# The first units of a feed-forward: a store behind the fetches, the third block early, a next unit's product moved up

## The chip, the cores and the metric

The kernel runs on one core of a Trainium2 chip. Its time is the device time of one execution in microseconds (us). The engines are TensorE (PE, with its weight loads as PEld), VectorE (DVE), ScalarE (ACT), GpSimd (POOL) and SyncE (SP), whose queue issues all the transfers spoken of here.

## The reference

One layer of a decoder over 2048 prompt tokens and 64 sample tokens, all in float32: an input projection, windowed attention and gated linear attention, an output projection with a residual, and a feed-forward with a squared ReLU. The change lies where the output projection ends and the feed-forward begins:

```
mix = jnp.einsum('bte,ed->btd', jnp.concatenate([attn.astype(x.dtype), gla_out], axis=-1), w_out)
x = x + rms_norm(mix, g_mix_post)
h = rms_norm(x, g_ffn_pre)
u = jax.nn.relu(jnp.einsum('btd,df->btf', h, w_up))
f = jnp.einsum('btf,fd->btd', u * u, w_down)
x = x + rms_norm(f, g_ffn_post)
```

w_up is 1024 x 4096, w_down 4096 x 1024.

## The kernel before

**Products.** A float32 product is made of three matmuls of a shorter type: each operand is split into a high half (a copy on ScalarE) and a low half (a subtraction on VectorE), and high x high, high x low and low x high are added. Both large products of the feed-forward also save one multiplication in eight: operands are cut into 2 x 2 quarters, sums of quarters are formed, and seven products take the place of eight. The seven blocks of activations are H1 to H7. A product with one of them is 12 matmuls of 128x128 on 128x512 (four slices of the inner dimension, three matmuls each).

**Stages.** The prompt is done in two halves of 1024 tokens (`sb` 0 and 1). For each half the up stage (`up`) runs 16 units (`fc` 0 to 15) of 256 columns of w_up; each forms its seven products and two products for the sample tokens, squares the features, and stores them to memory. Then the down stage (`down`) reads features and weight sums back and multiplies them (bank tiles `dn`).

**Rows.** `residual(i, ...)` finishes a block of 128 rows after the output projection: norm, residual, store to `x1_d` (L1423), norm, transposes on TensorE into two banks (`xnT`, L1523), copies out of them on ScalarE into a tile `ht` (L1528), four sums on VectorE (L1535), and a store of the sums to `h_d` (L1537). That store has 3584 pieces of 512 bytes. Row blocks come in the order 0, 4, 1, 5, ..., 10, 14, 11, 15; two of them share one `ht`, and all `ht` share one place, so the copies of block 11 wait until the store of the pair 10 and 14 has landed. Blocks 10, 14, 11 and 15 belong to the second half (`h_d[1]`); the last of them runs inside unit 0 of the first half (`last_rows`), where its transposes use the two banks that block 11's used.

**Unit 0.** H1 and H2 are kept in place. H5, H7 and H6 are fetched from `h_d[0]` as `hraw` (`fetch_h`, L1549) and split (`load_h`); H3 and H4 are fetched late into the place of their own low halves (L1824) and split there (`split_in_place`). The order of unit 0 is written out in `opening`: after each product p of UP_FIRST = (1, 0, 2, 8, 5, 7, 9, 6, 3, 4) stand the steps of that place (0 and 8 are the sample products, 9 their transposes). Later units use UP_ORDER = (1, 5, 7, 0, 6, 8, 3, 2, 9, 4).

**What sets the order.** `te`, `ac` and `dv` are wrappers that keep TensorE, ScalarE and VectorE in the order in which the program is written; their instructions all show as L130. Work on the bare engines (`split_copy`, L218 and L219, and the row blocks before the last) is placed between by the scheduler. The transfers stand on SP's queue, and `tc.issue_after` puts one behind another. Pools of memory are opened and released like a stack, and a tile that lies where an older one lay waits for that one's last reader.

**Names in the profile.** `ua` to `ue` are the banks of products; `s` are the split sums of weight quarters (`13` and `24` in the code), `t` those sums before the split, `w` the split quarters, `raw` the fetched weights, `st` the unit's features, `sam` the sample bank, `both` its copy, `samq` and `samp` the sample features, `rs`, `rt`, `o0s`, `o1s`, `o0t`, `o1t` the down stage's fetched and split operands. `load_up` fetches weights (L1576), `load_down` the second matrix (L1665).

Of the kernel before, what the change touches and what calls it, by code (L numbers as in the profile page):

```python
# [12 lines left out]
F32 = mybir.dt.float32  # L13
# [8 lines left out]
P = 128  # L22
# [31 lines left out]
H_EARLY, H_LATE = (1, 2), (5, 7, 6, 4, 3)  # L54
# [86 lines left out]
def hybrid_step_kernel(ctx: ExitStack, tc: tile.TileContext, I, O):  # L141
# [1266 lines left out]
    def mixed(i, banks, x, x1, junk, ssq, gpost, pool, scalar=nc.scalar, vector=nc.vector):  # L1408
# [14 lines left out]
        nc.sync.dma_start(x1_d[i], x[:n])  # L1423
# [72 lines left out]

    def residual(i, banks, tensor=nc.tensor, scalar=nc.scalar, vector=nc.vector):
# [21 lines left out]
        for h in range(2):  # L1519
# [8 lines left out]
            scalar.activation(ht[:, (6, 2)[h] if second else h], pt, AF.Copy)  # L1528
# [8 lines left out]
        nc.sync.dma_start(h_d[sb][:, kept, :, q], ht[:, kept])  # L1537
# [3 lines left out]
    def fetch_h(sb, p, home="h"):  # L1541
        h_raws[p] = []
        for k in range(0, KT // 2, 2):
# [5 lines left out]
            nc.sync.dma_start(raw, h_d[sb][:, p - 1, k : k + 2])  # L1549
            h_raws[p].append(raw)  # L1550

    def load_h(sb, p, scalar=nc.scalar, vector=nc.vector):
# [40 lines left out]
    for n, i in enumerate(B_ORDER[2:]):  # L1593
# [9 lines left out]
        if n != 1:  # L1603
            run(residual(*early.pop(0)))
# [18 lines left out]
    fetch_h(0, 6, "tmp")  # L1623
# [54 lines left out]

    def up(sb, fc, before, steps=iter(())):
# [5 lines left out]
        X, Z, Y, V = (bank([P, BT], kind, f"u{kind}_{sb}_{fc}") for kind in ("ab"[first], "c", "ba"[first], "de"[fc % 2]))  # L1685
        sam = bank([P, BT], "b", f"sam_{fc}") if sb == 0 else None
        place = []
# [7 lines left out]
        def product(p):  # L1695
            out = {1: X, 2: X, 5: Z, 3: Z, 7: V, 4: V, 6: Y}[p]
            hi, lo = H[p]
            for k in range(KT // 2):
                for u, (a, b) in enumerate(((0, hi), (0, lo), (1, hi))):
                    te.matmul(  # L1700
                        out, weight(sb, fc, p, a, k), b[:, k], start=p in (1, 5, 7, 6) and k + u == 0,
                        stop=k == KT // 2 - 1 and u == 2, skip_group_check=True,
                    )
# [4 lines left out]
        def taken(p):  # L1708
# [38 lines left out]
        for p in UP_FIRST if first else UP_ORDER:  # L1747
            if 0 < p < 8:
# [7 lines left out]
            if first:  # L1756
                opening(p, taken, ahead)
                if p == 3:
                    squared(s(6))
                continue  # L1760
            if p == 1:
                next(before, None)
                if fc or sb:
# [22 lines left out]
        if sb == 0:  # L1786
            sample_features(fc, sam)
# [401 lines left out]
```

## Time and profile before

| | us |
|---|---|
| median of 3 runs | 2207.52 (2206.16 to 2207.61) |
| the profiled execution | 2206.11 |
| its span, first to last instruction | 2204.0 |
| TensorE busy | 2163.2 (98%) |
| VectorE busy | 1531.4 (69%) |
| ScalarE busy | 1219.1 (55%) |

The mean granted clock of TensorE is 0.996 of full speed. A row in order of time gives start, length, engine, line, operation, the tile written and the tile read, shapes, a count where equal rows are merged, and in brackets the idle time before it and what ended that. Matmul rows overlap: a row of twelve is 2.9 us long, and the next begins 2.7 us after it.

### The profile page before, as it was taken

The page shows a single profiled execution, that of the slowest core. Times are in us where ns is not written, and L with a number is a line of the kernel's source. Part 1 is how long each engine was busy: PE and PEld are TensorE (multiplying, and loading weights), DVE is VectorE, ACT ScalarE, POOL GpSimd, SP SyncE. Part 2 cuts the span into 40 slices and gives each one's busy share as a digit, 9 for nine tenths or more (in the row PEclk, how much of TensorE's full clock was granted, in tenths as well). Part 3 has the DMA queues.
Part 4 walks back from the last instruction along what each step waited for, and adds up shares of the span by engine and source line. Part 5 has one row for each costly group of instructions (what it writes and reads, how often), then busy time and mean ns, then how long its engine had stood idle before and what let it go on. Part 6 is the DMA issues. An engine that isn't in the chain of part 4 may idle for free.

```text
span 2204.0 us, 34115 instructions
## 1 busy us (share of the span) xinstructions
PE 2163.2 (98%) x11784; PEld 1864.7 (85%) x11784; DVE 1531.4 (69%) x3101; ACT 1219.1 (55%) x2626; POOL 263.0 (12%) x418
## 2 busy tenths in 40 slices
PE   8999999999999999899999999999999999999998
PEld 7999989999998888688888887887888888888886
DVE  5888868777775665788888655547676666555566
ACT  5889867566664444555555544435444554444444
POOL 2566512121111100000000000000000000000000
PEclk9999999999999999999999999999999999999999
DMA  6344232214336665768777677758554334766685
GB/s 228 131 137 156 96 106 70 68 64 148 136 125 237 223 208 190 239 228 277 260 261 270 232 236 225 240 182 260 180 195 149 138 144 148 238 201 193 194 269 185
DMA packets 240185, 411.53 MB, mean 187 GB/s; under 512 B 25924, under 2 KB 142124, under 8 KB 235900
## 3 DMA queue, kind: packets, MB, share of 16 engines
q1 hardware_dynamic: 240012, 409.35, 55.9%
q8 instruction: 93, 1.52, 0.3%
q14 instruction: 80, 0.66, 0.1%
HBM read 265.82 MB, written 143.99 MB: 186 GB/s over the span
## 4 chain that ended last, share of the span: by engine, by line
PE 85%; DVE 6%; ACT 4%; DMA 2%; issue 1%; POOL 1%; SPq 0%; DVEq 0%; ACTq 0%; POOLq 0%
PE dn L130 26%; PE gproj L130 10%; PE uc L130 7%; PE ua L130 7%; PE out L1318 6%; PE proj L130 5%; PE ue L130 4%; PE ud L130 4%; PE ub L130 4%; PE av L130 1%; PE sam L130 1%; PE dsam L130 1%; PE o L130 1%; PE pT L130 1%; PE sc L130 1%
## 5 line engine op out<-in xcount | busy, mean ns | idle before, releaser
L130 PE MATMUL dn<-o0t,o0s 128*128 128x512 f32 x896 | 349.3, 390 | 2.8 <-DVE f L1891 1.5
L130 PE MATMUL dn<-o1t,o0s 128*128 128x512 f32 x896 | 349.5, 390 | 0.3 <-DVE o1t L219 0.2
L130 PE MATMUL dn<-o0t,o1s 128*128 128x512 f32 x896 | 349.4, 390 | 0.0
L219 DVE TENSOR_TENSOR o1s<-rs,o0s 128x512 fp32r<-128x512 f32 x224 | 154.7, 691 | 227.8 <-ACT o0s L218 223.7
L218 ACT ACTIVATE o0s<-rs 128x512 fp32r<-128x512 f32 x224 | 141.1, 631 | 305.5 <-PE dn L130 282.3
L130 PE MATMUL gproj<-wg,gxh 128*128 128x384 f32 x1024 | 272.5, 342 | 0.3 <-DVE gp_s L213 0.3
L130 ACT ACTIVATE st<-st 128x512 f32<-128x512 f32 x224 | 141.2, 630 | 140.7 <-DVE st L130 136.6
L130 PEld LDWEIGHTS dn<-o0t,o0s 128*128 128x128 f32 x896 | 168.3, 188 | 40.6 <-DVE f L1891 2.4
L130 PEld LDWEIGHTS dn<-o1t,o0s 128*128 128x128 f32 x896 | 168.2, 188 | 37.0 <-DVE o1t L219 1.1
L130 PEld LDWEIGHTS dn<-o0t,o1s 128*128 128x128 f32 x896 | 168.2, 188 | 35.0
L130 PEld LDWEIGHTS gproj<-wg,gxh 128*128 128x128 f32 x1024 | 183.8, 188 | 4.1 <-issue 3.1
L130 PE MATMUL uc<-H,s 128*128 128x512 f32 x768 | 186.8, 391 | 0.4 <-DVE s L130 0.4
L130 PE MATMUL gproj<-wg,gxl 128*128 128x384 f32 x576 | 186.0, 340 | 0.2 <-DVE gp_s L213 0.2
L130 PE MATMUL ua<-H,w 128*128 128x512 f32 x744 | 179.2, 390 | 0.0
L130 PEld LDWEIGHTS uc<-H,s 128*128 128x128 f32 x768 | 142.9, 188 | 31.2 <-DVE s L130 0.8
L130 PEld LDWEIGHTS ua<-H,w 128*128 128x128 f32 x744 | 139.7, 188 | 29.5
L1318 PE MATMUL out<-wo,mt 128*128 128x512 f32 x680 | 158.6, 392 | 0.0
L219 DVE TENSOR_TENSOR o1t<-rt,o0t 128x512 fp32r<-128x512 f32 x224 | 153.5, 685 | 7.0 <-ACT o0t L218 6.9
L208 POOL TENSOR_TENSOR frs<-rs_v,half 128x1 f32<-128x1 f32 (+1 forms) x13 | 10.1, 787 | 1214.4 <-DVE rs_v L206 694.5
L1318 PEld LDWEIGHTS out<-wo,mt 128*128 128x128 f32 x680 | 126.5, 188 | 26.1
L218 ACT ACTIVATE o0t<-rt 128x512 fp32r<-128x512 f32 x224 | 138.3, 618 | 8.9 <-DMA rt<-t_d 7.2
L130 DVE TENSOR_TENSOR st<-st 128x512 f32<-128x512 f32 x160 | 110.6, 692 | 27.0 <-ACT st L130 22.6
(405 smaller groups left out, 4322.3 us busy)
## 6 DMA issues: line engine op xcount, KB each, us to landing
s_d<-st SPq DMA_DIRECT2D x32, 1792.0 KB, 8.7
rs<-s_d SPq DMA_DIRECT2D x224, 256.0 KB, 2.8
raw<-in_w_up SPq DMA_DIRECT2D x64, 512.0 KB, 4.3
rt<-t_d SPq DMA_DIRECT2D x128, 256.0 KB, 4.1
rt<-in_w_down SPq DMA_DIRECT2D x96, 256.0 KB, 3.1
t<-in_w_down SPq DMA_DIRECT2D x64, 256.0 KB, 4.0
t_d<-t SPq DMA_DIRECT2D x32, 512.0 KB, 3.2
hraw<-h_d SPq DMA_DIRECT2D x20, 512.0 KB, 5.1
```

The costliest lines, as they stand in the source:

```text
L130: ins = call(*a, **k)
L208: nc.gpsimd.tensor_tensor(out, v[:n], e, op=ALU.pow)
L218: nc.scalar.activation(hi, src, AF.Copy)
L219: vector.tensor_tensor(lo, src, f32(hi), op=ALU.subtract)
L1318: te.matmul(banks[c], x, w[:, c * 512 : (c + 1) * 512], start=k + u == 0, stop=k == KT - 1 and u == len(products) - 1,)
```

## The change

**Transfers.** The two fetches of H6 now stand right behind those of H7, then unit 1's weights, and only then the store of the row pair 10 and 14. H3 is fetched early, into free parts of unit 0's feature tile, and split from there; only H4 is still fetched into its own place. The fetches of w_down go behind the store of the last row pair. On SP's queue before, from the fetches of H7 on (`hraw_7`; `h_d_99` is the second half's store, `x_d` the row store, `t_0` and `t_1` w_down):

```order
L1549 DMA hraw_7_2_10959<-h_d_98 128x1024
L1576 DMA raw_0_1_10978<-in_w_up 128x4x256 [waits DMAHW5_49,DVE_49]
L1576 DMA raw_0_1_10979<-in_w_up 128x4x256 [waits DMAHW6_49,DVE_49]
L1549 DMA hraw_6_0_10961<-h_d_98 128x1024 [waits DMAHW7_49,PE_49]
L1537 DMA h_d_99<-ht_10785 3584x1x128 [waits DVE_49]
L1549 DMA hraw_6_2_10963<-h_d_98 128x1024 [waits DMAHW1_49]
L1423 DMA x_d_175<-bx_10982 128x1024 [waits DMAHW2_49,DVE_49]
L1665 DMA t_0_11165<-in_w_down 128x2x256 [waits DMAHW3_49]
```

And now, at the same place:

```order
L1559 DMA hraw_7_2_10956<-h_d_98 128x1024
L1559 DMA hraw_6_0_10958<-h_d_98 128x1024 [waits DMAHW5_49,PE_49]
L1559 DMA hraw_6_2_10960<-h_d_98 128x1024 [waits DMAHW6_49]
L1597 DMA raw_0_1_10975<-in_w_up 128x4x256 [waits DMAHW7_49,DVE_49]
L1597 DMA raw_0_1_10976<-in_w_up 128x4x256 [waits DVE_49]
L1547 DMA h_d_99<-ht_10785 3584x1x128 [waits DMAHW1_49,DVE_49]
L1423 DMA x_d_175<-bx_10981 128x1024 [waits DMAHW2_49,DVE_49]
L1842 DMA st_0_10980<-h_d_98 128x1024 [waits DMAHW3_49,PE_49]
L1842 DMA st_0_10980<-h_d_98 128x2x512 [waits DMAHW4_49]
L1869 DMA H_0_11121<-h_d_98 128x1024 [waits DMAHW6_49,DMAHW5_49,DVE_49]
```

The store moved behind the second fetch of H6 and the weights, and H3's two fetches stand where w_down's stood. Each transfer has one of eight semaphores in turn; the store's is DMAHW0 before and DMAHW1 now.

**Unit 0 on the engines.** The transposes of row block 15 stand one product earlier, ahead of product 7 (`ud`) and no longer behind it. The copies of block 11 have a fixed place on ScalarE (`late_copies`), as before ahead of the sample copy. Unit 1's first product stands behind unit 0's product 6, and the high and low half of its weights ahead of that. Block 7's split is cut in two, the high halves ahead of row block 15's steps and the low halves behind them. On TensorE before:

```order
L130 MATMUL ud_0_11002<-H_0_10993,s_0_0_10974 128x512
L130 MATMUL ud_0_11002<-H_0_10994,s_0_0_10974 128x512
L130 MATMUL ud_0_11002<-H_0_10993,s_0_0_10975 128x512
L130 MATMUL xnT_0_11098<-ident,x_15_10986 128x128 [waits DVE_49,PE_49,Activation_49]
L130 MATMUL xnT_0_11098<-ident,x_15_10986 128x128 x3
L130 MATMUL xnT_1_11104<-ident,x_15_10986 128x128 [waits PE_49,Activation_49]
```

And now:

```order
L130 MATMUL uc_0_10997<-H_0_10965,s_0_0_10971 128x512
L130 MATMUL uc_0_10997<-H_0_10966,s_0_0_10971 128x512
L130 MATMUL uc_0_10997<-H_0_10965,s_0_0_10972 128x512
L130 MATMUL xnT_0_11091<-ident,x_15_10985 128x128 [waits DVE_49,PE_49,Activation_49]
L130 MATMUL xnT_0_11091<-ident,x_15_10985 128x128 x3
L130 MATMUL xnT_1_11097<-ident,x_15_10985 128x128 [waits PE_49,Activation_49]
L130 MATMUL xnT_1_11097<-ident,x_15_10985 128x128 x3
L130 MATMUL ud_0_10999<-H_0_10992,s_0_0_10971 128x512
```

They moved from behind `ud` to behind `uc`. On ScalarE the place of block 11's copies now, between the weights of unit 1 and the sample copy:

```order
L130 ACTIVATE w_0_1_11051<-raw_0_1_10975 128x1024 [waits DMAHW7_49]
L130 ACTIVATE ht_10908<-xnT_0_10909 128x512 [waits DMAHW1_49]
L130 ACTIVATE ht_10908<-xnT_1_10914 128x512
L130 ACTIVATE both_11065<-sam_11000 128x256 [waits PE_49]
L130 ACTIVATE s_0_0_11067<-t_0_0_10962 128x1024 [waits DVE_49]
L130 ACTIVATE H_0_11071<-hraw_6_0_10958 128x1024 [waits DMAHW5_49]
L130 ACTIVATE H_0_11071<-hraw_6_2_10960 128x1024 [waits DMAHW6_49]
```

Their wait is for the store's semaphore; block 6's split moved from around them to behind the sums.

**Sums in two steps.** The first half of the sample features of unit 0 is taken before its last products. In units 1 to 15 of the first half the pair of squares of feature 3 stands behind the sample copy `both` and no longer ahead of it.

**Memory.** H3's and H4's pools are opened in the other order, so H4's low half lies where H3's lay. In the down stage the tile `o0t` lies there. On ScalarE at the entrance to the down stage before:

```order
L130 ACTIVATE both_13851<-sam_13769 128x256 [waits PE_49]
L218 ACTIVATE o0s_6_0_13994<-rs_6_0_13982 128x512 [waits DMAHW5_49]
L218 ACTIVATE o0t_6_0_13998<-rt_6_0_13984 128x512 [waits DMAHW2_49,PE_49]
L218 ACTIVATE o0s_6_1_14002<-rs_6_1_13986 128x512 [waits DMAHW6_49]
L130 ACTIVATE st_15_13791<-st_15_13791 128x512 [waits DVE_49]
```

And now:

```order
L218 ACTIVATE o0s_6_2_14018<-rs_6_2_13990 128x512 [waits DMAHW7_49]
L130 ACTIVATE st_15_13791<-st_15_13791 128x512 [waits Activation_49]
L130 ACTIVATE st_15_13791<-uX_15_13765 128x512 [waits PE_49]
L130 ACTIVATE st_15_13791<-st_15_13791 128x512 [waits Activation_49]
L130 ACTIVATE samq_13899<-sam_13769 128x128 [waits PE_49]
L218 ACTIVATE o0t_6_0_13998<-rt_6_0_13984 128x512 [waits DMAHW2_49,PE_49]
L218 ACTIVATE o0t_6_1_14006<-rt_6_1_13988 128x512 [waits DMAHW3_49]
```

The first `o0t` moved from behind the sample copy to behind the last features. The diff, cut to its core:

```diff
-H_EARLY, H_LATE = (1, 2), (5, 7, 6, 4, 3)
+H_EARLY, H_LATE = (1, 2), (5, 7, 6, 3, 4)
...
-            scalar.activation(ht[:, (6, 2)[h] if second else h], pt, AF.Copy)
+            copy = (ht[:, (6, 2)[h] if second else h], pt, AF.Copy)
+            if i == B_ORDER[-2]:
+                late_copies.append(copy)
+            else:
+                scalar.activation(*copy)
...
+            if out == 6 and i == B_ORDER[-1]:
+                yield
         kept = slice(2 * (sb == 0), 7)
-        nc.sync.dma_start(h_d[sb][:, kept, :, q], ht[:, kept])
+        if i == B_ORDER[-3]:
+            yield
+        latest_store[:] = [nc.sync.dma_start(h_d[sb][:, kept, :, q], ht[:, kept])]
...
+    def split_apart(sb, p):
+        h_place(sb, p)
+        parts = [([t[:, 2 * n : 2 * n + 2] for t in H[p]], raw) for n, raw in enumerate(h_raws.pop(p))]
+        for (hi, _), raw in parts:
+            ac.activation(hi, raw, AF.Copy)
+        yield
+        for (hi, lo), raw in parts:
+            dv.tensor_tensor(lo, raw, f32(hi), op=ALU.subtract)
+        yield
...
-        if n != 1:
+        if i == B_ORDER[-1]:
+            waiting_rows = residual(*early.pop(0))
+            run(waiting_rows, 5)
+        elif n != 1:
             run(residual(*early.pop(0)))
...
-                squared(s(3))
+                if first or sb:
+                    squared(s(3))
             elif p == 8:
                 both.append(U["sam"].tile([P, FC], F32, tag="sam", name=f"both_{fc}", bufs=1))
                 ac.activation(both[0], sam[:, :FC], AF.Copy)
+                if not first:
+                    squared(s(3))
...
         if p == 1:
             taken(p)
+            next(last_rows)
+            loaded = placing[0]
+            for n, raw in enumerate(h_raws[3]):
+                with tc.issue_after(loaded.ins):
+                    loaded = nc.sync.dma_start(raw, h_d[0][:, 2, 2 * n : 2 * n + 2])
+            next(seventh)
         elif p == 0:
             next(last_rows)
+            sums_24(0, 0, dv)
         elif p == 2:
             taken(p)
-            next(last_rows)
+            ahead("a")
+            for copy in late_copies:
+                ac.activation(*copy)
+        elif p == 8:
+            taken(p)
+            split_sums(0, 0, 24, ac, dv)
             run(load_h(0, 6, ac, dv))
             U.pop("tmp").release()
...
+            ahead("s13")
+            run(load_h(0, 3, ac, dv))
+            h_place(0, 4)
+            loaded = None
+            for k in range(0, KT // 2, 2):
+                with tc.issue_after(loaded.ins) if loaded else nullcontext():
+                    loaded = nc.sync.dma_start(f32(H[4][1][:, k : k + 2]), h_d[0][:, 3, k : k + 2])
             with tc.issue_after(loaded.ins):
-                load_up(0, 2)
+                latest_store[:] = [load_up(0, 2)]
+        elif p == 7:
+            taken(p)
+            next(last_rows)
+            split_in_place(4)
         elif p == 9:
             taken(p)
+            ahead("13")
+            run(last_rows)
         elif p == 6:
-            split_in_place(3)
-            ahead("a")
+            next_X.append(bank([P, BT], "a", "uX_0_1"))
+            up_product(0, 1, 1, next_X[0])
             taken(p)
-            split_in_place(4)
-            run(last_rows)
-            for half in range(2):
-                load_down(0, half)
         elif p == 3:
-            ahead("s13")
-            ahead("13")
+            with tc.issue_after(latest_store[0].ins):
+                for half in range(2):
+                    load_down(0, half)
         else:
             ahead("s24")
             ahead("24")
+            split_up(0, 1, 1, ac, dv)
...
-    load_up(0, 1)
+    with tc.issue_after(sixth):
+        second_up = load_up(0, 1)
+    with tc.issue_after(second_up.ins):
+        run(waiting_rows)
+    st_first = U["st0"].tile([P, 7, BT], F32, tag="st", name="st_0_0", bufs=1)
+    h_raws[3] = [st_first[:, 4:6], st_first[:, 2:7:4]]
     next(last_rows)
-    run(load_h(0, 7, ac, dv))
+    seventh = split_apart(0, 7)
+    next(seventh)
...
-            for p in (3, 4, 7, 6):
+            for p in (4, 3, 7, 6):
```

More of the change, by code (lines that the diff above doesn't have):

```diff
@@ L1548, in fetch_h @@
             raw = pool.tile([P, 2, BT], F32, tag=tag, name=f"hraw_{sb}_{p}_{k}", bufs=1)
-            nc.sync.dma_start(raw, h_d[sb][:, p - 1, k : k + 2])
+            fetched = nc.sync.dma_start(raw, h_d[sb][:, p - 1, k : k + 2])
             h_raws[p].append(raw)
+        return fetched
     def load_h(sb, p, scalar=nc.scalar, vector=nc.vector):
@@ L1695, in product @@
         def product(p):
[L1696 to L1703, printed above, removed]
+            up_product(sb, fc, p, {1: X, 2: X, 5: Z, 3: Z, 7: V, 4: V, 6: Y}[p])
         def add(out, a, b, op=ALU.add):
@@ L1747, in up @@
         for p in UP_FIRST if first else UP_ORDER:
-            if 0 < p < 8:
+            if (sb, fc, p) == (0, 1, 1):
+                pass
+            elif 0 < p < 8:
                 product(p)
@@ L1759, in up @@
                     squared(s(6))
+                elif p == 6:
+                    next(features)
                 continue
@@ L1785, in up @@
         add(4, s(5), s(0))
-        if sb == 0:
-            sample_features(fc, sam)
+        run(features)
         def end():
```

33 lines of the change are left out of this document (18 added, 15 removed).

## The prediction

> **What bounds the kernel now.** I read the busy table first, then stages by windows, then TensorE's waits where its busy time falls short of the stage, and last the rows in order of time there.
>
> ```profile
> PE 2163.2 (98%) x11784; PEld 1864.7 (85%) x11784; DVE 1531.4 (69%) x3101; ACT 1219.1 (55%) x2626; POOL 263.0 (12%) x418
> ```
>
> TensorE is the bound, with 41 us idle in all. By stage (columns: stretch, length, then busy time of PE, PEld, DVE, ACT, POOL, the granted clock, DMA share, GB/s): the first two units of the feed-forward, the next thirteen, the last one of the first half.
>
> ```profile
> 885.62:943.36 57.74, 49.33 (x215) 38.74 (x214) 42.66 (x54) 30.95 (x48) 1.95 (x2) 0.94 0.72 235
> 943.36:1220.09 276.73, 276.73 (x1327) 232.00 (x1326) 231.94 (x378) 149.17 (x249) 0.00 (x0) 1.00 0.74 253
> 1220.09:1241.38 21.29, 21.29 (x104) 17.85 (x103) 10.74 (x17) 11.21 (x22) 0.00 (x0) 1.00 0.64 219
> ```
>
> A unit without stalls takes 276.73/13 = 21.29 us. Units 0 and 1 hold two of these and eight transposes (0.8 us, below), 43.4 us, but take 57.74: 14.3 us are lost there, and nothing in the thirteen units behind. So 14.3 us is the ceiling of any gain. TensorE's five longest waits in that stretch (last column the longest one):
>
> ```profile
> PE ua L130 <- ACT s L130: 3.0, 1, 3.0
> PE sam L130 <- ACT both L130: 2.0, 2, 1.7
> PE ud L130 <- ACT H L130: 1.8, 1, 1.8
> PE ud L130 <- DVE H L130: 0.8, 1, 0.8
> PE ua L130 <- DVE s L130: 0.5, 1, 0.5
> ```
>
> They sum to 8.1 us. Much of the rest is a halved clock (same columns as above):
>
> ```profile
> 901.43:904.85 3.42, 0.96 (x3) 0.52 (x4) 2.26 (x4) 2.59 (x5) 0.00 (x0) 1.00 0.87 266
> 904.85:908.26 3.41, 3.41 (x9) 2.63 (x9) 2.49 (x3) 2.87 (x3) 0.00 (x0) 0.50 1.01 402
> 911.67:915.08 3.41, 0.99 (x3) 0.64 (x4) 1.77 (x2) 2.52 (x3) 0.00 (x0) 1.00 0.00 1
> 915.08:918.50 3.42, 3.42 (x10) 2.65 (x9) 3.35 (x6) 0.00 (x0) 0.00 (x0) 0.50 0.02 5
> 938.97:942.39 3.42, 2.05 (x10) 1.75 (x11) 2.73 (x4) 3.35 (x7) 0.00 (x0) 1.00 0.61 195
> ```
>
> Twice a stretch with TensorE 28% busy is followed by one at clock 0.50, which costs 3.41 x 0.5 = 1.7 us each; a stretch 60% busy is not.
>
> **The fetches, the store and the moved transposes.** In time order (start, length, engine, line, what it writes and reads; in brackets the idle time before it and what ended it):
>
> ```profile
> 866.79 0.55 SPq L1537 DMA_DIRECT2D h_d<-ht  x1
> 874.90 1.09 ACT L1528 ACTIVATE ht<-xnT 128x512 f32<-128x512 f32 x2 [1.92 <-DMA h_d<-ht]
> ...
> 887.20 0.53 SPq L1537 DMA_DIRECT2D h_d<-ht  x1
> 887.78 6.58 SPq L1549 DMA_DIRECT2D hraw<-h_d  x1
> ...
> 892.20 1.12 PE L130 MATMUL sam<-w,xsT 128*128 128x256 f32 x8
> 893.15 2.91 PE L130 MATMUL uc<-H,s 128*128 128x512 f32 x12
> 895.90 2.89 PE L130 MATMUL ud<-H,s 128*128 128x512 f32 x12
> 896.72 1.09 ACT L1528 ACTIVATE ht<-xnT 128x512 f32<-128x512 f32 x2 [1.05 <-DMA h_d<-ht]
> 898.58 1.06 ACT L130 ACTIVATE H<-hraw 128x1024 fp32r<-128x1024 f32 x1 [0.78 <-DMA hraw<-h_d]
> 898.63 1.03 PE L130 MATMUL xnT<-ident,x 128*128 128x128 f32 x8
> ```
>
> Before, the second fetch of block 6 sat 6.58 us in the issue behind the store of row block 14, so its split came at 898.58 and with it the sums on which TensorE waited 3.0 us. After, both fetches stand ahead of the store and land about 890; that wait goes. What is late next is ScalarE's copies of row block 11 out of their banks: they write the tile which that store reads, so they start when it lands, 896.72 before. They were harmless; now the transposes of row block 15, which use the same two banks, stand one product earlier on TensorE, where it arrives at 895.90. A new wait is made.
>
> When does the store land (S)? Another store with little ahead of it took 874.90 - 866.79 = 8.1 us, which from 887.20 gives 895.3. This one took 9.5. Ahead of it now come 0.52 MB more, against the slack in these rows:
>
> ```profile
> 883.00:887.20 4.20, 4.20 (x24) 3.56 (x23) 4.20 (x7) 2.78 (x6) 0.00 (x0) 1.00 0.81 247
> 887.20:896.70 9.50, 9.50 (x51) 8.12 (x50) 7.50 (x10) 4.22 (x7) 1.95 (x2) 1.00 1.01 295
> 880.00:883.00 3.00, 3.00 (x14) 2.44 (x13) 3.00 (x5) 2.19 (x3) 0.00 (x0) 1.00 1.02 403
> ```
>
> 0.52 MB at the 403 GB/s that fetches reached is 1.3 us; 0.19 x 4.20 = 0.8 us of it fits where the DMA engines were not full. I take S = 896.7 + 0.6 = 897.3, between 895.3 and 896.7 + 1.8 = 898.5 (0.52 MB at 295).
>
> **From S to unit 2.** Every step behind the copies stands in one order on ScalarE and VectorE, so I sum it from S with these rows:
>
> ```profile
> 902.26 1.06 ACT L130 ACTIVATE s<-t 128x1024 fp32r<-128x1024 f32 x1 [2.35 <-DVE t L130]
> 913.30 2.36 DVE L130 TENSOR_TENSOR H<-H,H 128x1024 fp32r<-128x1024 f32 x2 [2.31 <-ACT H L130]
> 915.58 2.74 DVE L130 TENSOR_TENSOR ht<-ht 128x512 f32<-128x512 f32 x4
> ...
> 939.92 0.36 ACT L130 ACTIVATE both<-sam 128x256 f32<-128x256 f32 x1
> 941.13 1.29 ACT L130 ACTIVATE st<-st 128x512 f32<-128x512 f32 x2
> ```
>
> A VectorE instruction on 128x1024 takes (915.58 - 913.30)/2 = 1.14 us in a row, one on 128x512 about 0.67.
> - ScalarE: the two copies, the sample copy, the high half of the 2-and-4 sum: done at S+2.3.
> - VectorE then runs eight instructions of 1.14 and nine of 0.67 without a gap (s, block 6, the 1-and-3 sums of unit 1, block 3, block 4, sums of rows and features): S+17.4. ScalarE's pair of squares (1.29) and the sample copy: S+18.9. VectorE's four behind these: S+21.1. ScalarE's high half of unit 1's 2-and-4 sum, S+22.1, VectorE's low half (2.36 - 1.14 = 1.22), S+23.4.
> - TensorE: transposes done at S+1.55 (two copies, four transposes), then seven products at 898.63 - 895.90 = 2.73, sample work 0.95 + 0.15: it stands at unit 1's product 6 at S+21.75, runs two matmuls and waits until S+23.4, 1.2 us. Ten matmuls, 2.3: S+25.7. Sample work and two products: S+32.1.
> - The next sample copy has VectorE's six instructions, the pair of squares, three more on VectorE and two of ScalarE's ahead of it: S+32.95, so TensorE waits 0.85 again, where it waited 1.7. Then 0.15 + 2.73: unit 2 starts at S+35.9 = 933.2. Before it did so at 943.36, where the second window above begins: 10.2 us saved.
>
> Parts that come to nothing: block 3's fetch into the feature tile, behind one row store (1.57 MB together, 3.9 us at 403 GB/s), is there at about S+4 and split at S+5.7. Block 4's is issued when block 6's low half is done, S+5.8, since it lies where block 6 was fetched to. The queue is idle then, so I take the least landing time of such fetches (row below): the halves are there at S+10 and S+11.2, and the chain above has VectorE at block 4 from S+11.1. At the median 1 us, at the most 2.2 us go into the chain. Unit 1's first product, moved up, costs its 2.73 in either place and covers block 3's split. The fetches of the second weight matrix go behind the last row store at about S+16 and are read a unit later. The split of block 7 in two parts puts row block 15 earlier; the transposes wait for S anyway.
>
> ```profile
> DMA to landing us min/median/max: 4.1/5.1/6.3
> ```
>
> The wait at the transposes is 897.3 + 0.6 - 895.9 = 2.0 us, with a second of 0.4. Whether it halves the clock the rows above leave open: 42% busy lies between 28% and 60%. If it does, 1.7 us fall between S+1.6 and S+21.7, and the waits of 1.2 and 0.85 take them up.
>
> [...]
>
> **The way into the second product.** The first operand of the down stage, o0t, now lies where block 4's low half lies, which TensorE reads last, and no longer on block 3's.
>
> ```profile
> 1234.81 0.37 ACT L130 ACTIVATE both<-sam 128x256 f32<-128x256 f32 x1
> 1235.92 0.62 ACT L218 ACTIVATE o0t<-rt 128x512 fp32r<-128x512 f32 x1
> 1237.06 0.68 DVE L219 TENSOR_TENSOR o1t<-rt,o0t 128x512 fp32r<-128x512 f32 x1
> 1238.41 0.38 PE L130 MATMUL sam<-ident,both 128*128 128x128 f32 x2
> 1238.54 2.99 PE L130 MATMUL ue<-H,w 128*128 128x512 f32 x12
> 1241.38 0.39 PE L130 MATMUL dn<-o0t,o0s 128*128 128x512 f32 x1
> 1243.18 0.50 PE L130 MATMUL dn<-o0t,o0s 128*128 128x512 f32 x1 [0.27 <-DVE samq L130]
> ```
>
> ScalarE can begin it only when the product at 1238.54 has read that block, about 1241.4: 0.62, then 0.68 on VectorE, and the second matmul of the stage starts 1.4 us late. The wait of 0.3 that stood there goes. Net +0.9, between 0 (were the tile read earlier) and +1.5.
>
> **Sum.** -10.2 + 0.9 = -9.3 on the profiled run's own 2206.1 us (its span of 2204.0 and what lies around it): 2196.8. That run lies 1.4 below the median of 2207.52, on the level of the fastest of three; I add half of it: 2197.5.
>
> **Rivals.**
> - *S does not bind so late.* With S = 895.3, 2 us more come off: 2195.5. For it: a like store took 8.1 us. Against it: that one had an idle queue ahead.
> - *The store shares the engines with what is issued behind it.* Then S waits also for the row store and block 3's fetch, 1.57 MB at 295 GB/s = 5.3 us: S = 902.6, 2202.1, and with one halved stretch that is not covered 2203.8. For it: the store's 9.5 us against 8.1. Against it: the fetch stuck behind the store landed 1.9 us after it, so the queue served in order. [...]
> - *It gets slower.* The pair of squares of feature 3 is moved behind the sample copy in fifteen units. Three sums on VectorE and the tile's store stand behind those squares. If that put each of the fourteen units from unit 2 on off its 21.29 us, it decides from (9.3 + 4.4)/14 = 1.0 us a unit; at 1.2 the time is 2197.5 + 16.8 = 2214. Against it: the copy comes earlier, and in unit 15 it stood at 1234.81 for transposes at 1238.41, 3.2 us to spare.
> - *The change moves waits and removes none*: the 2.0 + 0.4 + 1.2 + 0.85 + 0.9 us above turn out double, 5 us more, and a halved stretch shows: 2204, no change. For it: VectorE is without a gap over 15 us of the chain, so each delay adds up.
>
> **Numbers.** The forecast has 0.60, the early store 0.14, the shared engines 0.13, no gain 0.07, slower 0.06. What a measurement tells from no change is 0.2%, 4.4 us: faster means under 2203.1. The forecast, the early store and two thirds of the third case are faster: 0.83; same 0.11; slower 0.06. The range: from S at 895.3 with no loss into the down stage (2194) to the shared engines (2203).
>
> **What would show it.** Right: TensorE's waits name the copies ht at the transposes (about 2 us), VectorE's s in unit 1 (1.2), the sample copy (0.9) and o0t and o1t at the first dn; no wait on s or H in unit 0; unit 2 starts near 933. Wrong: the store landing after 900, a wait on H of block 4, or units 2 to 14 off 21.29 us.

## The result, and the profile after

| | median us | ratio to the kernel before, 95% interval |
|---|---|---|
| before | 2206.96 (2204.75 to 2209.49) | |
| changed | 2201.93 (2198.14 to 2204.60) | 0.9974 [0.9966, 0.9982] |

The change makes the kernel 5.0 us faster at the medians. The profiled execution took 2200.13 us, its span 2198.2. The busy table of the changed kernel:

```profile
PE 2158.6 (98%) x11784; PEld 1861.8 (85%) x11784; DVE 1532.1 (70%) x3101; ACT 1220.7 (56%) x2626; POOL 261.8 (12%) x418
```

By stage (same columns as before: units 0 and 1, then the next thirteen units):

```profile
885.41:937.82 52.41, 46.37 (x216) 37.75 (x214) 41.99 (x54) 30.72 (x48) 1.08 (x2) 0.97 0.79 256
937.82:1214.50 276.68, 276.68 (x1327) 232.00 (x1326) 231.96 (x377) 150.70 (x249) 0.00 (x0) 1.00 0.74 253
```

Units 0 and 1 take 52.41 us, where they took 57.74; a unit behind them takes 21.28, as it did. 9.0 us (52.41 - 43.4) are still lost there. The waits of TensorE, in the first two units and at the entrance to the down stage:

```profile
PE uc L130 <- ACT st L130: 2.8, 1, 2.8
PE xnT L130 <- ACT ht L130: 2.3, 1, 2.3
PE ub L130 <- DVE s L130: 0.5, 1, 0.5
PE ub L130 <- ACT s L130: 0.4, 1, 0.4
...
PE dn L130 <- ACT o0t L218: 0.7, 1, 0.7
PE dn L130 <- DVE o1t L219: 0.2, 1, 0.2
```

Five of the six are those that the prediction names, at nearly its sizes. The longest, 2.8 us at uc, is not among them, and the wait for the sample copy, which it does name, isn't there. Rows in order of time, the wait at the transposes and then a selection from the second half of unit 1 on TensorE, ScalarE and VectorE:

```profile
898.20 1.15 PE L130 MATMUL xnT<-ident,x 128*128 128x128 f32 x8 [2.34 <-ACT ht L130]
...
921.39 2.57 PE L130 MATMUL ub<-H,s 128*128 128x512 f32 x10 [0.53 <-DVE s L130]
921.60 0.31 ACT L130 ACTIVATE samp<-samq 128x128 fp32r<-128x128 f32 x1
923.80 1.11 PE L130 MATMUL sam<-w,xsT 128*128 128x256 f32 x8
924.64 0.68 DVE L130 TENSOR_TENSOR st<-st,ud 128x512 f32<-128x512 f32 x1
925.36 1.29 ACT L130 ACTIVATE st<-st 128x512 f32<-128x512 f32 x2 [3.45 <-DVE st L130]
926.56 0.58 ACT L130 ACTIVATE st<-uX 128x512 f32<-128x512 f32 x1
927.03 0.59 ACT L130 ACTIVATE st<-uc 128x512 f32<-128x512 f32 x1
927.67 4.61 PE L130 MATMUL uc<-H,s 128*128 128x512 f32 x12 [2.77 <-ACT st L130]
930.58 0.36 ACT L130 ACTIVATE both<-sam 128x256 f32<-128x256 f32 x1
932.12 2.89 PE L130 MATMUL uX<-H,w 128*128 128x512 f32 x12
934.85 0.38 PE L130 MATMUL sam<-ident,both 128*128 128x128 f32 x2
937.82 2.43 PE L130 MATMUL uX<-H,w 128*128 128x512 f32 x10
```

Product 3 of unit 1 writes the bank (uc) that product 5 wrote before, so it must wait until ScalarE has copied that out (`st<-uc`, 927.03). That copy and the one of uX stand on ScalarE behind unit 0's last pair of squares (925.36), and that pair waits 3.45 us for the end of unit 0's sums on VectorE (924.64). So TensorE, ready at 924.9, begins at 927.67. Its twelve matmuls then take 4.61 us, since the clock fell (columns as in the stages above; the clock is the third number from the end):

```profile
923.80:927.20 3.40, 1.11 (x9) 0.90 (x7) 2.01 (x5) 1.81 (x4) 0.00 (x0) 1.00 1.01 326
927.20:930.60 3.40, 2.93 (x7) 2.35 (x8) 2.82 (x5) 2.35 (x4) 0.00 (x0) 0.57 1.10 430
```

The second of these windows starts a little ahead of the halved stretch and shows 0.57; the stretch itself, at 0.50, runs from 927.68 to 931.09.

### The profile page after: what moved, and what is told of

Read it like the earlier page. It is cut to its first block, busy times and chain, and to the rows that moved or that the text cites. A ratio compares the mean times of both kernels' runs of the same rounds, so it can differ in the third digit from the quotient of the medians.

```text
span 2198.2 us, 34114 instructions
## 1 busy us (share of the span) xinstructions
PE 2158.6 (98%) x11784; PEld 1861.8 (85%) x11784; DVE 1532.1 (70%) x3101; ACT 1220.7 (56%) x2626; POOL 261.8 (12%) x418
## 4 chain that ended last, share of the span: by engine, by line
PE 85%; DVE 6%; ACT 4%; DMA 3%; issue 1%; POOL 1%; SPq 0%; DVEq 0%; ACTq 0%; POOLq 0%
PE dn L130 26%; PE gproj L130 10%; PE uc L130 8%; PE uX L130 7%; PE out L1318 6%; PE proj L130 5%; PE ue L130 4%; PE ud L130 4%; PE ub L130 4%; PE sam L130 1%; PE dsam L130 1%; PE av L130 1%; PE o L130 1%; PE pT L130 1%; PE sc L130 1%
## 5 line engine op out<-in xcount | busy, mean ns | idle before, releaser
L130 PE MATMUL uX<-H,w 128*128 128x512 f32 x768 | 185.2, 390 | 0.0
L130 PEld LDWEIGHTS uX<-H,w 128*128 128x128 f32 x768 | 144.0, 188 | 30.3
```

Source lines behind the costliest of these rows:

```text
L130: ins = call(*a, **k)
```

## The experiments

Each kernel is the changed one with one edit, unless more is said. S is the start of ScalarE's copies of block 11 (`ht<-xnT`), which wait for the row pair's store. The place where unit 0 starts in the span differs between profiles by 4.8 us (884.7 to 889.5, all of it from stages ahead of the change), so the table gives distances inside the stage. They are worked out from the rows of the store's issue, of the copies, of unit 2's first product and of product 3 of unit 1 (the twelve matmuls on uc). The ratio is to the kernel before, run beside it; that kernel's own median was between 2206.43 and 2207.26 in the four groups of runs, so medians from two groups compare to about 1 us.

| kernel | median us | ratio [95%] | store's issue to S | S to unit 2 | matmuls on uc |
|---|---|---|---|---|---|
| before | 2206.96 | | 9.5 | 46.6 | 3.0 |
| changed | 2201.93 | 0.9974 [0.9966, 0.9982] | 10.6 | 40.3 | 4.61 |
| changed, again | 2201.66 | 0.9972 [0.9961, 0.9982] | 9.6 | 40.4 | 4.61 |
| copies first | 2198.28 | 0.9963 [0.9950, 0.9977] | 9.0 | 35.5 | 2.91 |
| old places | 2200.65 | 0.9974 [0.9965, 0.9983] | 10.7 | 40.0 | 4.61 |
| transposes back | 2200.90 | 0.9977 [0.9967, 0.9987] | 9.7 | 38.7 | 3.04 |
| store in the middle | 2198.75 | 0.9963 [0.9950, 0.9975] | 8.7 | 38.7 | 3.04 |
| third block late | 2201.76 | 0.9974 [0.9963, 0.9985] | 9.3 | 40.2 | 4.43 |
| product not moved | 2201.44 | 0.9975 [0.9966, 0.9984] | 8.9 | 38.4 | 3.02 |
| third block late, old places | 2204.45 | 0.9988 [0.9980, 0.9997] | 9.8 | 44.2 | 4.62 |
| squares back | 2201.49 | 0.9975 [0.9965, 0.9985] | 10.5 | 40.5 | 4.60 |
| copies first, old places | 2195.14 | 0.9953 [0.9937, 0.9969] | 10.8 | 35.7 | 2.91 |
| the same, store in the middle | 2194.81 | 0.9944 [0.9931, 0.9956] | 8.6 | 35.3 | 2.91 |
| copies first, old places, own place | 2192.64 | 0.9938 [0.9925, 0.9951] | | 36.1 | 2.91 |

**Copies first.** Is the bank copy what the prediction missed? In unit 1 the second half of unit 0's end (the squares and the store) goes behind the copies of unit 1's first two banks:

```diff
-                deque(before, 0)
+                if (sb, fc) != (0, 1):
+                    deque(before, 0)
...
+            if (sb, fc, p) == (0, 1, 5):
+                deque(before, 0)
```

> Against the changed kernel. Theory 1 (product 3 of unit 1 waits for the copy of product 5 out of its bank, and that copy stands on ScalarE behind unit 0's squares): with the copies of unit 1's first two banks ahead of those squares the wait of 2.8 us at uc falls to about 1, since the copies still need the store of the last row pair, whose queue was free again at 922.0 and which should land 2.4 to 3 us later; the stretch at clock 0.57 behind it goes; 3.3 us faster, 1.8 if the clock still falls; unit 2 starts between 934.5 and 936. Rival (VectorE's row of work up to unit 2 sets its start, and the wait for the bank is only where it shows): less than 0.5 us.

3.6 us faster at the medians and 2.4 by the ratios. The intervals of the ratios overlap, so the answer rests on the trace, where unit 2 starts 35.5 us after S instead of 40.3. ScalarE and TensorE in this kernel:

```profile
922.25 0.60 ACT L130 ACTIVATE st<-uX 128x512 f32<-128x512 f32 x1 [0.72 <-DMA h_d<-ht]
922.74 0.59 ACT L130 ACTIVATE st<-uc 128x512 f32<-128x512 f32 x1
924.37 2.91 PE L130 MATMUL uc<-H,s 128*128 128x512 f32 x12
...
932.84 1.52 PE L130 MATMUL uX<-H,w 128*128 128x512 f32 x6
```

The last row pair's store landed earlier than I took it to (at 922.25, 0.65 us after its queue was free at 921.60), so the wait goes altogether and not down to 1 us, and the matmuls run at full clock. Unit 2 starts 35.5 us after S. The prediction had 35.9.

**Old places.** H_LATE and the order of release as they were.

```diff
-H_EARLY, H_LATE = (1, 2), (5, 7, 6, 3, 4)
+H_EARLY, H_LATE = (1, 2), (5, 7, 6, 4, 3)
...
-            for p in (4, 3, 7, 6):
+            for p in (3, 4, 7, 6):
```

> Against the changed kernel. Theory (o0t now lies on the block that TensorE reads last): with the two blocks in their old places the waits of 0.7 and 0.2 us at the first matmuls of the down stage go; from the start of unit 2 to the seventh matmul of the down stage it took 300.87 us instead of 299.82, so 1.05 us faster. Rival: a wait deeper in the down stage, which was 1.46 us before and is 0.19 now, comes back with the old places; no change, within 0.3. No change in units 0 and 1 by either.

From unit 2 to the seventh matmul of the down stage: 299.76 us (940.41 to 1240.17), 1.1 less than the 300.87 of the changed kernel. Three further kernels with the old places have 299.76 to 299.85 there, seven more with the new ones 300.88 to 300.92. (One more with the old places, copies first with the store behind the fetches, has 301.62: its profiled execution waits 2.1 us at the seventh matmul of the down stage.) So the theory holds in the trace. The median, 1.3 lower, is too near to its scatter to show it alone. The wait deeper in the down stage belongs to neither: it was 0.2, 0.9 and 1.4 us in three profiles with the new places.

**Transposes back.** Row block 15's transposes behind product 7 again.

```diff
         elif p == 5:
             taken(p)
-            next(last_rows)
             close_pools(R)
...
         elif p == 7:
             taken(p)
             next(last_rows)
+            next(last_rows)
             split_in_place(4)
```

> Against the changed kernel, with row block 15's transposes behind product 7 again. Theory (everything up to unit 1's product 6 is set from S on ScalarE and VectorE): the wait of 2.3 us at xnT goes, one of about the same length shows at product 6 of unit 0 (ua, for the low halves of s or H), and unit 2 starts where it did: within 0.5 us. Rival (the new wait at the transposes is paid in full): 2.3 us faster.

Waits of TensorE in this kernel:

```profile
PE uc L130 <- ACT st L130: 2.8, 1, 2.8
PE ua L130 <- DVE H L130: 1.0, 1, 1.0
PE ub L130 <- DVE s L130: 0.5, 1, 0.5
PE ub L130 <- ACT s L130: 0.3, 1, 0.3
PE ua L130 <- ACT H L130: 0.3, 1, 0.3
```

The wait at the transposes is gone, waits at ua (1.3 us) stand in its place, and unit 2 starts 38.7 us after S against 40.3. The 1.6 us between these is the clock and not the transposes, as the row of product 3 shows: it has the same gap ahead of it as in the changed kernel, and begins 30.1 us after S in both.

```profile
930.00 3.04 PE L130 MATMUL uc<-H,s 128*128 128x512 f32 x12 [2.77 <-ACT st L130]
```

The median is 1.0 lower, within its scatter. The new wait that the prediction priced at 2.0 us costs nothing by itself.

**Store in the middle.** The transfers in the old order: the store between the two fetches of H6.

```diff
...
-    sixth = fetch_h(0, 6, "tmp").ins
+    sixth = fetch_h(0, 6, "tmp", (0,)).ins
...
     with tc.issue_after(second_up.ins):
         run(waiting_rows)
+    with tc.issue_after(latest_store[0].ins):
+        fetch_h(0, 6, "tmp", (2,))
```

> The changed kernel with the transfers in the old order: first half of H6, unit 1's weights, the row pair's store, second half of H6. Theory of the prediction (S sets the chain, and H6's second half lands at about 898.5, when ScalarE wants it only at 900.7): not slower, 0 to 0.9 us faster by an S that is that much earlier. Rival (the reorder is what takes the wait of 3.0 us away): that wait comes back, 3.0 us slower.

The wait of 3.0 us does not come back: the second fetch sits 4.82 us in the issue behind the store, and ScalarE, held by S, splits it only at 897.16, without idling for it.

```profile
886.30 0.53 SPq L1547 DMA_DIRECT2D h_d<-ht  x1
886.88 4.82 SPq L1559 DMA_DIRECT2D hraw<-h_d  x1
894.98 1.09 ACT L130 ACTIVATE ht<-xnT 128x512 f32<-128x512 f32 x2 [1.27 <-DMA h_d<-ht]
897.16 2.02 ACT L130 ACTIVATE H<-hraw 128x1024 fp32r<-128x1024 f32 x2
```

So the first item in the change's name, taken back alone, costs nothing. The kernel is 3.2 us faster than the changed one at the medians (the intervals of the ratios overlap), more than I allowed: in its profile S comes 8.7 us after the issue, and the clock does not fall (uc 3.04).

**Changed, again.**

> The changed kernel once more, beside the three runs after it. The wait of 2.8 us at uc is the same in the changed kernel and in two variants of it that leave it in, but the stretch of halved clock behind it (1.6 us) showed in two of four profiles. If it depends on where the gap lies in the 3.41 us stretches of the clock, unit 2 starts 38.7 us after S without it or 40.3 us with it, and nothing between. S itself lay 9.0 to 10.7 us behind the store's issue in four kernels whose transfers up to there are the same; the same range again.

S lay 9.6 us behind the issue, unit 2 40.4 behind S, with uc at 4.61 us. Of the eight profiles with the gap of 2.7 to 2.8 us, six show the fall of the clock and two do not. In one of the six (third block late, uc 4.43) the halved stretch reaches into the next product (3.14 us instead of 2.90). That the place of the gap against the 3.41 us stretches decides it is not shown; it stays my estimate, and the last section has the figures that speak for it.

**Third block late.** H3 fetched into its own place, ahead of H4, and split there.

```diff
-            loaded = placing[0]
-            for n, raw in enumerate(h_raws[3]):
-                with tc.issue_after(loaded.ins):
-                    loaded = nc.sync.dma_start(raw, h_d[0][:, 2, 2 * n : 2 * n + 2])
...
-            run(load_h(0, 3, ac, dv))
-            h_place(0, 4)
-            loaded = None
-            for k in range(0, KT // 2, 2):
-                with tc.issue_after(loaded.ins) if loaded else nullcontext():
-                    loaded = nc.sync.dma_start(f32(H[4][1][:, k : k + 2]), h_d[0][:, 3, k : k + 2])
+            loaded = placing[0]
+            for q in (3, 4):
+                h_place(0, q)
+                for k in range(0, KT // 2, 2):
+                    with tc.issue_after(loaded.ins):
+                        loaded = nc.sync.dma_start(f32(H[q][1][:, k : k + 2]), h_d[0][:, q - 1, k : k + 2])
+            split_in_place(3)
```

> The changed kernel with the third block fetched late, into its own place, just ahead of the fourth. Theory (of the parts, it is the early fetch of the third block that lets VectorE run from S without a gap): the fetches can be issued when row block 15's transposes or block 6's low half are done, 899.5 to 903.4, and land 4.1 us later or more, 904 to 908.5, where VectorE wants them at 904.5: waits on H show at product 3 or 4, and unit 2 starts 1 to 4 us later from S than the 38.7 (or 40.3) of the changed kernel. Rival (the gain is from the moved product and the order of the sums): no more than 0.5 us.

The theory falls: 40.2 us from S to unit 2, and the same median. The fetch was issued at 900.41, as soon as row block 15's transposes were done, and ScalarE waited 0.28 us for it.

**Product not moved.** Unit 1's first product back in unit 1.

```diff
-            next_X.append(bank([P, BT], "a", "uX_0_1"))
-            up_product(0, 1, 1, next_X[0])
             taken(p)
...
-            if (sb, fc, p) == (0, 1, 1):
-                pass
-            elif 0 < p < 8:
+            if 0 < p < 8:
```

> The changed kernel with unit 1's first product back in unit 1. Theory (VectorE's row from S sets unit 1's product 6, and the product costs 2.73 us of TensorE in either place): TensorE comes to product 3 of unit 0 at 904.9 and waits about 2 us for the low half of H3 (906.9) and about 1 for H4, then as before from product 6 on; within 0.5 us of the changed kernel. Rival (the moved product is worth its own 2.73 us): that much slower.

The same median. TensorE waits 0.5 us for H3 and 1.0 for H4 instead, and comes to product 6 late enough not to wait there. The gap at uc shrinks to 1.8 us, with no fall of the clock behind it.

**Third block late, old places.** Both edits above. The third block's low half then lies where H6 was fetched to, as before the change.

> The changed kernel with the third block fetched late and the blocks in their old places, so that the third block's fetch can't start before block 6's low half is done, as before the change. Theory (the early fetch alone was worth nothing because the new places alone free the third block's place soon enough, at S + 1.8; with neither, the fetch starts at S + 5.8 and lands from S + 10 on, its low halves are done 3 to 4 us later than in the changed kernel, and VectorE's row shifts by that): unit 2 starts 41.7 to 42.7 us after S instead of 38.7, 1.6 more if a stretch of halved clock falls there; with the 1.05 us that the old places save at the down stage 2 to 3 us slower than the changed kernel. Rival (third block and places carry nothing of the gain): 1 us faster, by the down stage alone.

2.5 to 2.8 us slower than the two medians of the changed kernel, as expected. SP's queue, TensorE and VectorE in it:

```profile
904.65 1.76 SPq L1865 DMA_DIRECT2D H<-h_d  x4
909.77 2.51 DVE L130 TENSOR_TENSOR H<-H,H 128x1024 fp32r<-128x1024 f32 x2 [3.94 <-ACT H L130]
909.79 0.50 PE L130 MATMUL uc<-H,s 128*128 128x512 f32 x1 [0.68 <-ACT H L130]
```

The fetch starts at S + 5.9, VectorE idles 3.94 us at H3, and unit 2 starts 44.2 us after S, 42.6 without the fallen clock. So the third block does carry part of the gain, but by either of two edits: the early fetch, or the exchange of places that lets a late fetch start early enough. Each makes the other unnecessary, which is why taking back one alone showed nothing.

**Squares back.** The squares of feature 3 ahead of the sample copy in all units.

```diff
-                if first or sb:
-                    squared(s(3))
+                squared(s(3))
...
-                if not first:
-                    squared(s(3))
```

> The changed kernel with the squares of feature 3 ahead of the sample copy again in all units. Theory (the copy had 4 us to spare in unit 1 and 3.2 in the later ones, the pair takes 1.3): within 0.5 us of the changed kernel, units 2 to 14 at 21.28 us each. Rival 1 (the move is what took away the wait of 1.7 us at the sample copy): 1.3 to 1.7 us slower. Rival 2 (the move delays the sums behind the squares in each unit): faster.

The same median, and 276.72 us for the next thirteen units (939.22 to 1215.94), which is 21.29 each: nothing either way.

**Copies first, old places, store in the middle.** Three of the edits above together.

> The changed kernel with unit 1's copies ahead of unit 0's squares, the transfers in the old order (store between the two halves of H6) and the blocks in their old places. By the traces of these parts alone: unit 2 starts at S + 35.5 and S lies 1.9 us earlier (8.7 us behind the store's issue), which is 6.6 us less from unit 0 to unit 2 than in the changed kernel, and 1.05 less into the down stage: 7.7 us faster, 2194.3. If the parts overlap (an earlier S makes TensorE wait elsewhere, for the copies of the last row pair's store): 5 us, 2197.

6.9 us faster than the changed kernel run beside it, 12.5 than the kernel before: the parts nearly add up (7.7).

**Copies first, old places.** The same with the store behind the fetches.

> The changed kernel with unit 1's copies ahead of unit 0's squares and the blocks in their old places; the store stays behind the fetches. Theory (the store behind both fetches lands 1 us later than between them, 9.7 us behind its issue on the mean against 8.6): 1 us slower than the kernel that also has the old order of transfers, 2196. Rival (the order of the transfers is worth nothing): the same, 2195.

2195.14 against 2194.81, with intervals that overlap widely: nearer to the rival. Once the copies are first, the runs can't tell the order of the transfers. Its profiled execution is a long one (2205.22 us, with a wait of 2.1 us at the seventh matmul of the down stage that no other profile has, and a clock of 0.99, 0.97, 0.99 and 0.99 in four windows from 600 to 1545 us where the kernel with the own place has 1.00 in each), so only its distances from S are used. The clock fell behind the wait at the transposes; the two rows there take 1.97 and 3.82 us, where they take 1.14 and 3.01 in the changed kernel, again:

```profile
902.51 1.97 PE L130 MATMUL xnT<-ident,x 128*128 128x128 f32 x8 [2.61 <-ACT ht L130]
904.14 3.82 PE L130 MATMUL ud<-H,s 128*128 128x512 f32 x12
```

From the first of them to the next product it took 5.29 us instead of 3.76, 1.5 more. Unit 2 still starts 35.7 us after S, where it is 35.3 and 35.5 in the two kernels with the copies first and no such fall there. So most of the 1.5 us is taken up by waits that get shorter, as the prediction said of this case.

**Own place.** The same, with block 11's copies in a tile of their own, in a place that w_down's fetches use later, and a store of its own for it (VectorE's sums read their first two parts from there):

```diff
-            for copy in late_copies:
-                ac.activation(*copy)
+            late_low.append(keep.tile([P, 2, KT // 2, P], F32, tag="t0", name="ht_low", bufs=1))
+            for h, pt in enumerate(late_copies):
+                ac.activation(late_low[0][:, h], pt, AF.Copy)
...
+        if i == B_ORDER[-1]:
+            nc.sync.dma_start(h_d[sb][:, :2, :, q], late_low[0])
+            kept = slice(2, 7)
```

> The changed kernel with unit 1's copies ahead of unit 0's squares, the old places, and block 11's copies in a place of their own, so that they need not wait until the row pair's store has landed. Theory (S governs the start of unit 2 through these copies): they start right behind the split of unit 1's weights, 6.2 us after unit 0's first sample product begins, and unit 2 starts 35.4 us after that, whatever the store takes; 8 us faster than the changed kernel, 2 to 3 faster than the same kernel without the own place. Rival (the store holds something else up, above all block 15's copies, or VectorE cannot start its row earlier): not faster than without the own place.

2192.64 us, 0.9938 [0.9925, 0.9951] of the kernel before, and the fastest of all. Its profile, the copies and then units 0 and 1 (columns as in the stages above):

```profile
896.42 1.07 ACT L130 ACTIVATE ht_low<-xnT 128x512 f32<-128x512 f32 x2
...
887.55:932.50 44.95, 44.34 (x215) 36.59 (x214) 40.30 (x53) 28.05 (x44) 1.08 (x2) 1.00 0.87 287
```

The copies start 6.0 us after unit 0's first sample product, unit 2 36.1 us after them, 0.7 more than expected since ScalarE now waits 0.66 us for VectorE's sums. Units 0 and 1 take 44.95 us; without stalls they would take 43.4. The interval of the ratio overlaps that of the kernel without the own place, so the gain of 2.5 us over it rests on the trace too: the copies start 6.0 us after the sample product where they started 7.3 to 9.5 after it, and unit 2 follows them at the same distance. That S governed the start of unit 2 is what the column of S to unit 2 shows.

## Why the prediction was right, and where it fell short

It gave 2197.5 and a range of 2194 to 2203, faster; the time was 2201.93. The direction and the chain from S hold. The gain is 5.0 us at the medians and 6.0 between the two profiles, where -9.3 was the sum. That the time still lies inside the range is luck in part: its upper end was set by a rival that did not occur, the shared engines. Two figures of the prediction also start from 2196.8 instead of the 2197.5 that it forecasts. From 2197.5 the shared engines give 2202.8 and not 2202.1, and S at 895.3 with no loss into the down stage 2194.6 and not 2194; neither moves the argument.

- *S.* Forecast 897.3, bounds 895.3 to 898.5; measured 897.55. In the other profiles with the same transfers ahead of it S lay 8.9 to 10.8 us behind the issue: no early store (8.1) and no shared engines (15).
- *The wait at the transposes.* 2.0 and 0.4 forecast, one of 2.34 measured. No fall of the clock followed (1.00 from 899.9 to 903.3). The prediction held this open. Here the gap lay across two of the 3.41 us steps counted back from the fall at 927.68 (last section), from 893.55 and from 896.96, with TensorE busy 68% and 64% of them.
- *Block 4's fetch.* S + 10 and S + 11.2 forecast; ScalarE took the halves at S + 9.6 and S + 11.5.
- *Unit 1's product 6.* S + 23.4 forecast, S + 23.8 measured, with 0.4 + 0.5 us of waits against 1.2.
- *From there to unit 2: the step that failed.* The prediction let TensorE run "sample work and two products: S+32.1" and then wait 0.85 for the sample copy. The first of these two products needs product 5 copied out of the same bank. Before the change no wait is listed there, so I did not price it (its sign is shown below). Now it costs 2.77 us, and 1.7 for the fallen clock behind it (4.45 instead of 2.73 to the next product, 927.67 to 932.12), while the wait for the sample copy (0.85) vanishes. With 0.55 carried from product 6 and 0.2 of roundings that is the whole of 40.3 - 35.9. The copies-first kernel takes just this out and starts unit 2 at S + 35.5.
- *The way into the down stage.* +0.9 forecast, +1.05 measured (300.87 against 299.82), by the waits it named.
- *The rest of the span.* From the seventh matmul of the down stage to the end it took 959.51 us, 1.3 less than before. In the other kernels with the same code there it took 959.3 to 961.2, and 964.1 in the long execution named above, so this is not shown to be the change's.
- *Parts costed at nothing.* The moved product, the moved transposes and the squares, each taken back alone, change nothing, as said. The rival by the squares of feature 3 is out. The rival "moves waits and removes none" came nearest: it had a surplus (5 us and a halved stretch) of the size that came (4.4 us, the stretch included), put on terms that were right already. The shared engines gave about the time that was measured, by a mechanism that didn't occur.
- *What gave the gain.* I ascribed the end of the 3.0 us wait to the fetches that now stand ahead of the store. By the run with the old order that was not needed. Shown is a share of 2.5 to 2.8 us, 3.9 from S to unit 2, for the third block by its early fetch or its new place. With both taken back 2.7 us stay (2204.45 against 2207.12 of the kernel before beside it). In the profiles 2.2 of them lie in units 0 and 1 (55.57 us against 57.74), where the kernel before has two halved stretches and this one has one (product 3 of unit 1 takes 4.62 us); at 1.7 us each that can be most of it. They were not split further, so which parts of the change carry them stays open.

The profile of before held the sign of the failed step, in two rows that the prediction doesn't show, ScalarE's copy of that bank and TensorE's product 3 in unit 1:

```profile
932.27 0.59 ACT L130 ACTIVATE st<-uc 128x512 f32<-128x512 f32 x1
932.91 3.04 PE L130 MATMUL uc<-H,s 128*128 128x512 f32 x12
```

The copy ends (932.86) just as the product begins. No wait is listed, but there is no slack either for a TensorE that comes earlier.

## What to carry to other kernels

List, for each operation that is moved earlier, every reader that must empty the bank or tile it writes, and where that reader stands in its engine's order, also where the profile of before shows no wait for it: a wait that was covered has no row. Find the one event from which a stage is set (here a store's landing) and measure from it; between profiles the distances stay within 0.5 us, a halved stretch of the clock (1.6 us) apart, while the times scatter by 6. An edit whose removal changes nothing may still carry the gain, if a second edit covers for it; take back both.

## What the runs showed of the hardware

The same gap on TensorE, 2.7 to 2.8 us, was followed by a stretch of halved clock in six of eight profiles and not in two, a difference of 1.6 us. In the kernel with the old places, half-microsecond windows show where such a stretch begins and ends:

```profile
930.22:930.72 0.50, 0.50 (x2) 0.39 (x3) 0.50 (x2) 0.00 (x0) 0.00 (x0) 0.74 1.09 352
...
933.72:934.22 0.50, 0.50 (x4) 0.41 (x3) 0.50 (x1) 0.00 (x0) 0.00 (x0) 0.85 1.08 459
```

A clock of 0.74 and of 0.85 (third number from the end) puts the ends at 930.46 and 933.87, 3.41 us apart. Apart from the last 10 us of the span, the clock fell at 37.83, 112.92, 904.82 and 915.06 us in the profile of the kernel before, for 3.41 us each time; the times between these falls are 22, 232 and 3 times 3.4133 us. In that of the changed kernel it fell at 36.80 and 927.68, 261 times 3.4133 us apart. So in these two profiles I count in steps of this length from the falls. Some of these steps, and for the old places the 3.41 us ahead of the fall at 930.46, with how long TensorE was busy in them by the rows of the profiles, in which the ends of matmuls are modelled:

| kernel | step | TensorE busy in it, us | share | clock in the next step |
|---|---|---|---|---|
| before | 34.42 to 37.83 | 0.87 | 25% | 0.50 |
| before | 109.51 to 112.92 | 1.24 | 36% | 0.50 |
| before | 723.91 to 727.32 | 1.83 | 54% | 1.00 |
| before | 901.40 to 904.82 | 0.93 | 27% | 0.50 |
| before | 911.64 to 915.06 | 0.97 | 28% | 0.50 |
| before | 938.95 to 942.36 | 2.02 | 59% | 1.00 |
| changed | 33.39 to 36.80 | 0.83 | 24% | 0.50 |
| changed | 722.88 to 726.29 | 1.73 | 51% | 1.00 |
| changed | 893.55 to 896.96 | 2.31 | 68% | 1.00 |
| changed | 896.96 to 900.38 | 2.18 | 64% | 1.00 |
| changed | 924.27 to 927.68 | 0.65 | 19% | 0.50 |
| old places | 927.05 to 930.46 | 0.65 | 19% | 0.50 |

In these rows the clock fell after 19% to 36% and stayed at 1.00 after 51% to 68%. The gap of 2.34 us at the transposes of the changed kernel lies across two steps, and no fall followed; those at uc in the changed kernel and in the one with the old places lie almost whole in one. The fall came 0.01 us after the gap in the changed kernel and 0.24 us after it in the one with the old places. In the one with the third block late I estimate 1.3 us from its rows: the product behind uc starts at 932.81 and takes 0.25 us longer than at full clock (2.98 instead of 2.73 to the next row), so a stretch of 3.41 us ends at about 933.3 and begins at about 929.9, and uc starts at 928.58.

In the two profiles without a fall every half-microsecond window around the gap shows a clock of 1.00 (922.00 to 936.00 with the transposes back, 917.02 to 931.02 with the store in the middle). That the gap lay across two steps there, as at the transposes of the changed kernel, is an estimate from these rows; where the steps lie in those two profiles is not shown.

A store of 3584 pieces of 512 bytes (1.84 MB) landed, by the copies that wait for it, 8.9 to 10.8 us after its issue in ten profiles of kernels whose transfers ahead of it are the same, and 9.6 and 10.6 us in two of the same kernel. What makes the difference is not known. Here, where the store sets the chain, that is 1.9 us of scatter in the start of S.
